# A last column tile computed by two halves of 176 tokens, each with its own norm and output

## Chip, core and metric

The kernel runs on one core of one Trainium2 chip. The metric is the time of one execution in device microseconds (us). Three runs before the change took 1801.14 us in the median (1799.97 to 1801.76).

## What is computed

One layer of a hybrid decoder for 1024 prompt tokens and 32 sample tokens (8 sequences of 4): an input projection shared by four branches, the branches themselves, an output projection with the residual, and a last RMS norm. The change touches only the end of this:

```python
mix = jnp.concatenate([y_ml, y_ssd, y_sc, y_rg], axis=-1)
y = x + mix @ w_out
...
x32 = x.astype(jnp.float32)
y = x32 * lax.rsqrt(jnp.mean(x32 * x32, axis=-1, keepdims=True) + EPS)
return (y * w.astype(jnp.float32)).astype(x.dtype)
```

D is 2048, so the norm of a token needs the token's value in all 2048 features before any of them can be stored.

## The kernel before

The data lie transposed: features on the 128 partitions (16 column tiles n of 128 features), the 1056 tokens along the free axis. `out_proj` (L1322) computes the tokens in two groups. The first has 704 tokens as two chunks of 352, the last has 352 (`GB`). For each of its 16 column tiles the last group's loop (L1404) loads the residual (`begin`, L1336), runs eight steps ke of six matmuls each, and ends with `fin` (L1343): residual added on VectorE (L1351), square on ScalarE (L1358), the squares summed into `acc` (L1359), and the tile scaled by the norm's weight (L1361).

**Three matmuls for one.** For f32 accuracy `mm6` (L278) uses split operands: xh and xl for the data, wh and wl for the weights, each kept in float32r. A step ke has two blocks of 128 rows and for each the lines L282, L283 and L284, every one with its own weight load. In the last group each matmul streams 352 columns.

**The weights.** `weights_list` (L225) lists every weight tile in the order of use. `w_load` (L247) issues the loads on SyncE (L252) into a ring of raw buffers, six in this stage; `w_split` (L255) makes wh with a copy on ScalarE (L264) and wl with a subtraction on VectorE (L265). Eight pairs of split buffers are in use in the last group, four of them regions of xl that are no longer needed. A pair is free again when the six matmuls that read it are done. `w_next` (L268) runs up to seven splits ahead, so the splits of a tile's ke 6 and ke 7 are placed while that tile computes. A raw buffer's next load is placed one split after the split that empties it, and waits for that split's subtraction.

**Order.** The program is written out by hand: each engine executes its instructions in the order in which the code emits them, and an instruction that waits holds up all behind it on that engine. Issuing a DMA occupies its engine's queue too.

**The end.** After the 48 matmuls of the last tile (n = 15) the norm follows once for all 352 tokens: the sum over the partitions of `acc` by matmuls with a column of 1/D (L1423), the last tile's residual and square (L1425, L1426, in two pieces of 128 and 224 tokens), its sum (L1428), square root (L1430), reciprocal (L1431), the result spread over the partitions by transposes into two banks (L1434), a copy of one of them for GpSimd (L1436). Then 16 multiplications, eleven on VectorE (L1443), four on GpSimd (L1441) and the last tile's own (L1439), and one output DMA for each on SyncE (L1444). The square root needs a table of ScalarE, loaded ahead of a dummy at L1419.

Of the kernel before, what the change touches and what calls it, by code (L numbers as in the profile page):

```python
# [12 lines left out]
AF = mybir.ActivationFunctionType  # L13
OP = mybir.AluOpType

D = 2048
KT = 16
TP = 1024
TS = 32
NT = TP + TS  # L20
# [7 lines left out]
GB = CH  # L28
# [80 lines left out]
class Build:  # L109
# [115 lines left out]
    def weights_list(self):  # L225
# [14 lines left out]
        for n in range(KT):  # L240
            for ke in range(8):
                lst.append((o, n, ke))
# [1079 lines left out]
    def out_proj(self):  # L1322
        V, S, G, P, Q = self.V, self.S, self.G, self.P, self.Q
        io = self.io
# [79 lines left out]
        for n in range(KT):  # L1404
# [5 lines left out]
            if n == KT - 1:  # L1410
                break
            fin(n, 1, [(b, w) for b, _, w in ch])

        nb = (GB + 127) // 128
        cut = [(i, slice(128 * i, min(GB, 128 * i + 128)), min(128, GB - 128 * i)) for i in range(nb)]
        tc, rc, mean = self.take(nb), self.take(nb), self.take(2)
# [3 lines left out]
        bs, bk = [self.mx() for _ in cut], self.pj()  # L1420
        y, t, b = ys[1], sq[0], ch[0][0]
        for i, ts, m in cut:
            P.matmul(bs[i][:m, 0:1], acc[1][:, ts], mean[:, 0:1], start=True, stop=False)  # L1423
        for ts in (slice(0, 128), slice(128, GB)):
            V.tensor_add(y[KT - 1][:, ts], b[:, ts], y[KT - 1][:, ts])  # L1425
            S.activation(t[:, ts], y[KT - 1][:, ts], AF.Square)  # L1426
        for i, ts, m in cut:
            P.matmul(bs[i][:m, 0:1], t[:, ts], mean[:, 0:1], start=False, stop=True)  # L1428
        for i, ts, m in cut:
            S.activation(tc[:m, i:i + 1], bs[i][:m, 0:1], AF.Sqrt, bias=self.eps[:m])  # L1430
        V.reciprocal(rc.ap, tc.ap)  # L1431
        bk2 = self.pj()
        for b, (i, ts, m) in [(b, x) for b in (bk, bk2) for x in cut]:
            P.transpose(b[:, ts], rc[:m, i:i + 1].to_broadcast([m, 128]), self.ident[:m, :m])  # L1434
        rb = self.take(GB)
        S.activation(rb.ap, bk2[:, :GB], AF.Copy)  # L1436
        for n in range(KT):
            if n == KT - 1:
                V.scalar_tensor_tensor(y[n], y[n], self.par("fnorm", n), rb.ap, op0=OP.mult, op1=OP.mult)  # L1439
            elif n % 3 == 2 and n < 14:  # L1440
                G.tensor_mul(y[n], y[n], rb.ap)  # L1441
            else:
                V.tensor_mul(y[n], y[n], bk[:, :GB])  # L1443
            Q.dma_start(io["y_out"][n, :, W[0]:NT], y[n])  # L1444
# [141 lines left out]
```

## Time and profile before

| what | value |
|---|---|
| median of three runs | 1801.14 us |
| the profiled execution | 1800.25 us |
| its span, first to last instruction | 1798.5 us |
| mean granted TensorE clock | 0.997 |
| last column tile (1776.58 to 1784.45) | 7.87 us |
| norm, to the first output's issue (1784.45 to 1787.77) | 3.32 us |
| first to last output's issue (1787.77 to 1795.76) | 7.99 us |
| from there to the end | 2.74 us |

Times in the trace count from the first instruction; the 1.75 us between span and execution lie around it. Engines are PE (TensorE; PEld are its weight loads), DVE (VectorE), ACT (ScalarE), POOL (GpSimd), SP (SyncE); a name with q (SPq, ACTq) is that engine's queue issuing a DMA. A merged row of the timeline gives start, length from the first start to the last end, the line, the operation and how many instructions it holds; in brackets stands how long the engine was idle ahead of it and who ended that. Matmuls overlap, so their spacing is read from starts, not from durations.

### The profile page before, as it was taken

What the parts mean: (1) busy time and instruction counts of PE and PEld (TensorE: products, weight loads), DVE (VectorE), ACT (ScalarE), POOL (GpSimd) and SP (SyncE); (2) the same over time, 40 slices, a digit from 0 to 9 for tenths busy, and PEclk for the clock granted to TensorE, in tenths of its full rate; (3) what the DMA queues carried; (4) which work ended last, traced back from release to release, by engine and by line L of the source; (5) the groups of instructions that cost most, each with busy time, mean ns of one, the idle gap of its engine ahead of it and who ended that gap; (6) DMA issues with size and microseconds to landing.
All of it is one profiled execution on the core that took longest, in us unless ns stands there. A gap on an engine that the chain in (4) does not pass through costs nothing.

```text
span 1798.5 us, 30156 instructions
## 1 busy us (share of the span) xinstructions
PE 1782.8 (99%) x11459; PEld 1752.9 (97%) x11459; DVE 910.8 (51%) x2018; ACT 531.7 (30%) x1263; POOL 182.9 (10%) x244
## 2 busy tenths in 40 slices
PE   9999999999999999999999999999999999999997
PEld 8899999999999999999999999999999999999997
DVE  4493454535435444765277556544763633333664
ACT  6522122212212111331144122212441432222453
POOL 1000102011011000320000003100000011110121
PEclk9999999999999999999999999999999999999998
DMA  9411213122122122332212233321123633332774
GB/s 341 146 55 50 78 49 90 50 71 74 58 68 62 53 59 71 91 80 67 80 42 60 63 78 92 69 84 57 57 61 92 202 111 94 94 92 86 216 246 152
DMA packets 141558, 168.19 MB, mean 94 GB/s; under 512 B 18220, under 2 KB 126196, under 8 KB 140900
## 3 DMA queue, kind: packets, MB, share of 16 engines
q1 hardware_dynamic: 135492, 145.36, 28.6%
q0 software_dynamic: 5184, 19.42, 2.8%
q8 instruction: 90, 1.47, 0.3%
q10 hardware_dynamic: 736, 1.48, 0.2%
q14 instruction: 56, 0.46, 0.1%
HBM read 144.35 MB, written 21.84 MB: 92 GB/s over the span
## 4 chain that ended last, share of the span: by engine, by line
PE 91%; issue 6%; DVE 1%; DMA 0%; SPq 0%; ACT 0%; POOL 0%; DVEq 0%; ACTq 0%; POOLq 0%
PE bank L282 29%; PE bank L284 28%; PE bank L283 28%; PE bank L1114 1%; PE bank L498 0%; PE bank L900 0%; PE bank L878 0%; PE bank L899 0%; PE bank L1108 0%; DMA arena<-in_x 0%; PE bank L902 0%; PE bank L1111 0%; PE bank L876 0%; DVE arena L1443 0%; PE bank L1196 0%
## 5 line engine op out<-in xcount | busy, mean ns | idle before, releaser
L282 PE MATMUL bank<-xh,wh 128*128 128x352 f32 x3328 | 1084.6, 326 | 0.5 <-DVE arena L593 0.4
L283 PE MATMUL bank<-xl,wh 128*128 128x352 f32 x3328 | 1072.0, 322 | 1.4 <-DVE xl L474 1.4
L284 PE MATMUL bank<-xh,wl 128*128 128x352 f32 x3328 | 1071.8, 322 | 0.5 <-DVE wl L265 0.5
L282 PEld LDWEIGHTS bank<-xh,wh 128*128 128x128 f32 x3328 | 625.4, 188 | 12.9 <-issue 10.1
L283 PEld LDWEIGHTS bank<-xl,wh 128*128 128x128 f32 x3328 | 626.0, 188 | 2.2 <-DVE xl L474 2.2
L284 PEld LDWEIGHTS bank<-xh,wl 128*128 128x128 f32 x3328 | 626.2, 188 | 1.2 <-DVE wl L265 1.2
L265 DVE TENSOR_TENSOR wl<-wr,wh 128x256 fp32r<-128x256 f32 x568 | 247.9, 447 | 407.2 <-ACT wh L264 404.8
L264 ACT ACTIVATE wh<-wr 128x256 fp32r<-128x256 f32 x568 | 227.1, 413 | 593.7 <-PE bank L283 529.2
L593 DVE TENSOR_TENSOR arena<-bank,arena 128x352 f32<-128x352 f32 x114 | 58.4, 523 | 73.3 <-PE bank L284 72.8
L1359 POOL TENSOR_TENSOR arena<-arena 128x352 f32<-128x352 f32 x39 | 36.8, 948 | 316.0 <-ACT arena L1358 315.8
L944 DVE SCALAR_TENSOR_TENSOR arena<-arena 128x1080 f32<-128x1080 f32 (+1 forms) x44 | 59.9, 1362 | 1.0
L265 DVE TENSOR_TENSOR wl<-arena,wh 128x256 fp32r<-128x256 f32 x72 | 31.5, 451 | 42.3 <-ACT wh L264 42.1
L1358 ACT ACTIVATE arena<-arena 128x352 f32<-128x352 f32 x44 | 21.9, 500 | 68.4 <-DVE arena L1351 66.5
L282 PE MATMUL bank<-xh,xl 128*128 128x352 f32 x128 | 41.5, 324 | 0.0
L284 PE MATMUL bank<-xh,xl 128*128 128x352 f32 x128 | 41.4, 324 | 0.0
L264 ACT ACTIVATE wh<-arena 128x256 fp32r<-128x256 f32 x72 | 28.7, 410 | 42.6 <-PE bank L283 39.9
L283 PE MATMUL bank<-xl 128*128 128x352 f32 x128 | 41.1, 321 | 0.0
L1351 DVE TENSOR_TENSOR arena<-bank,arena 128x352 f32<-128x352 f32 x47 | 24.0, 522 | 32.7 <-PE bank L284 32.6
L586 DVE TENSOR_TENSOR arena<-bank,arena 128x352 f32<-128x352 f32 x32 | 16.4, 522 | 42.4 <-PE bank L284 42.4
L399 DVE RECIPROCAL arena<-arena 128x352 f32<-128x352 f32 (+3 forms) x18 | 35.6, 1980 | 0.2
L474 DVE SCALAR_TENSOR_TENSOR xl<-arena,xh 128x1056 fp32r<-128x1056 f32 (+1 forms) x20 | 21.7, 1095 | 23.3 <-ACT xh L471 23.3
L932 POOL COPY arena<-arena 128x3 f32<-128x3 f32 (+1 forms) x16 | 5.1, 317 | 267.1 <-DVE arena L588 267.1
(340 smaller groups left out, 1253.7 us busy)
## 6 DMA issues: line engine op xcount, KB each, us to landing
wr<-in_w_in SPq DMA_DIRECT2D x438, 128.0 KB
wr<-in_w_out SPq DMA_DIRECT2D x172, 128.0 KB
arena<-in_w_out SPq DMA_DIRECT2D x84, 128.0 KB
arena<-in_xr SPq DMA_DIRECT2D x16, 512.0 KB
arena<-rowd SPq DMA_DIRECT2D x32, 256.0 KB
mixd<-arena POOLq DMA_DIRECT2D x15, 528.0 KB, 3.8
arena<-mixd SPq DMA_DIRECT2D x15, 528.0 KB
arena<-in_x SPq DMA_DIRECT2D x14, 528.5 KB
```

Of the source, the lines that this page charges most:

```text
L264: self.S.activation(h, r, AF.Copy)
L265: self.V.tensor_sub(l, r, h.bitcast(F32))
L282: self.P.matmul(bank[:, :n], wh[:, k, :], xh, start=first and k == 0, stop=False)
L283: self.P.matmul(bank[:, :n], wh[:, k, :], xl, start=False, stop=False)
L284: self.P.matmul(bank[:, :n], wl[:, k, :], xh, start=False, stop=last and k == 1)
L399: self.V.reciprocal(x[:, a:b], x[:, a:b])
L474: V.scalar_tensor_tensor(self.xl[:, k, ts], x, w, self.xh[:, k, ts].bitcast(F32), op0=OP.mult, op1=OP.subtract)
L593: V.tensor_mul(a[:, t0:t0 + CH], bank[:, :CH], rs[:, t0:t0 + CH])
L944: V.scalar_tensor_tensor(y[:, :n], a[:, i:i + n], w(i), y[:, :n], op0=OP.mult, op1=OP.add)
L1351: V.tensor_add(y[:, ts], b[:, :w], y[:, ts])
L1358: S.activation(t, y[:, ts], AF.Square)
L1359: (G if nacc[gr] < KT - 1 else V).tensor_add(a[:, ts], a[:, ts], t)
```

## The change

The last tile of the last group is computed twice over half the tokens: first all eight steps ke for tokens 0 to 175 of the group (h0 below), then all eight for tokens 176 to 351 (h1). The eight weight tiles are listed, loaded and split a second time for h1. The norm is a generator `norm(h, b)` with the same steps for 176 tokens (two cuts of 128 and 48), run up to the reciprocal after h1's ke 1, and the rest (transposes, multiplications, output DMAs of 88 KB) after h1's ke 3. The norm of h1 follows h1's matmuls. Outputs of h0 go out on SyncE, those of h1 on SyncE (even n) and on ScalarE (odd n). The memsets and the dummy square root with its table load now come ahead of the last tile's matmuls.

```diff
-        for n in range(KT):
+        for n in [*range(KT), KT - 1]:
             for ke in range(8):
                 lst.append((o, n, ke))
...
-        for n in range(KT):
+        for n in range(KT - 1):
             begin(n, 1)
...
+        begin(KT - 1, 1)
+        H = GB // 2
+        cuts = [(0, 128), (128, H)]
+        nb = len(cuts)
+        tc, rc, mean, rb = self.take(2 * nb), self.take(2 * nb), self.take(2), self.take(GB)
         V.memset(mean.ap, 1.0 / D)
         V.memset(tc.ap, 1.0)
         S.activation(rc[:, 0:1], tc[:, 0:1], AF.Sqrt)
...
+        def norm(h, b):
+            t = sq[h]
+            bs, bk, bk2 = [self.mx() for _ in cuts], self.pj(), self.pj()
+            for i, (u, v) in enumerate(cuts):
+                P.matmul(bs[i][:v - u, 0:1], acc[1][:, H * h + u:H * h + v], mean[:, 0:1], start=True, stop=False)
+            hs = slice(H * h, H * h + H)
+            V.tensor_add(y[KT - 1][:, hs], b[:, :H], y[KT - 1][:, hs])
+            S.activation(t[:, :H], y[KT - 1][:, hs], AF.Square)
+            for i, (u, v) in enumerate(cuts):
+                P.matmul(bs[i][:v - u, 0:1], t[:, u:v], mean[:, 0:1], start=False, stop=True)
+            for i, (u, v) in enumerate(cuts):
+                S.activation(tc[:v - u, nb * h + i:nb * h + i + 1], bs[i][:v - u, 0:1], AF.Sqrt, bias=self.eps[:v - u])
+            V.reciprocal(rc[:, nb * h:nb * h + nb], tc[:, nb * h:nb * h + nb])
+            yield
+            for bb in (bk, bk2):
+                for i, (u, v) in enumerate(cuts):
+                    P.transpose(bb[:, u:v], rc[:v - u, nb * h + i:nb * h + i + 1].to_broadcast([v - u, 128]),
+                                self.ident[:v - u, :v - u])
+            S.activation(rb[:, hs], bk2[:, :H], AF.Copy)
+            for n in range(KT):
...
+                (S if n % 2 and h else Q).dma_start(io["y_out"][n, :, W[0] + H * h:W[0] + H * h + H], y[n][:, hs])
+
+        hb = [self.pj(), self.pj()]
+        for h in range(2):
+            for ke in range(8):
+                w = self.w_next()
+                self.mm6(hb[h], *w, ke, W[0] + H * h, H, ke == 0, ke == 7)
+                if h and ke == 1:
+                    part = norm(0, hb[0])
+                    next(part)
+                elif h and ke == 3:
+                    for _ in part:
+                        pass
+        for _ in norm(1, hb[1]):
+            pass
```

In the changed kernel the norm's lines are L1426 (sum of `acc`), L1428 (residual), L1429 (square), L1431 (sum of the last tile), L1433 (square root), L1434 (reciprocal), L1438 (transposes), L1440 (copy), L1447, L1445 and L1443 (multiplications on VectorE, GpSimd, and the last tile's) and L1448 (output DMAs).

How the instructions stand on ScalarE from the end of tile 14 on, before (wr, wh and xl are the raw and split weight buffers, the number a buffer's; arena is working memory):

```order
L1361 ACTIVATE arena<-arena 128x352
L264 ACTIVATE xl<-wr_67 128x2x128
L264 ACTIVATE wh_77<-wr_68 128x256
L1419 ACT_TABLE_LOAD
L1419 ACTIVATE arena<-arena 128x1
L1426 ACTIVATE arena<-arena 128x128
L1426 ACTIVATE arena<-arena 128x224
```

The same place after the change:

```order
L1419 ACT_TABLE_LOAD
L1419 ACTIVATE arena<-arena 128x1
L264 ACTIVATE xl<-wr_67 128x2x128
L264 ACTIVATE wh_77<-wr_68 128x256
L264 ACTIVATE wh_71<-wr_69 128x256
L264 ACTIVATE wh_73<-arena 128x256
L264 ACTIVATE wh_75<-arena 128x256
L264 ACTIVATE xl<-wr_70 128x2x128
L264 ACTIVATE xl<-wr_67 128x2x128
L264 ACTIVATE xl<-wr_68 128x2x128
L264 ACTIVATE xl<-wr_69 128x2x128
L264 ACTIVATE wh_77<-arena 128x256
```

The table load and the dummy have moved ahead of the last tile's splits of ke 6 and ke 7 (the first two L264), and the eight splits of h1 follow them. Next on ScalarE comes L1429, the square of h0. On VectorE stands the matching order; after the change, from the first split of h1 on (bank_83 holds h0, bank_85 its spread factors):

```order
L265 TENSOR_TENSOR wl_72<-wr_69,wh_71 128x256
L265 TENSOR_TENSOR wl_74<-arena,wh_73 128x256
L265 TENSOR_TENSOR wl_76<-arena,wh_75 128x256
L265 TENSOR_TENSOR xl<-wr_70,xl 128x2x128
L265 TENSOR_TENSOR xl<-wr_67,xl 128x2x128
L265 TENSOR_TENSOR xl<-wr_68,xl 128x2x128
L265 TENSOR_TENSOR xl<-wr_69,xl 128x2x128
L265 TENSOR_TENSOR wl_78<-arena,wh_77 128x256
L1428 TENSOR_TENSOR arena<-bank_83,arena 128x176
L1434 RECIPROCAL arena<-arena 128x2
L1447 TENSOR_TENSOR arena<-arena,bank_85 128x176 x11
L1443 SCALAR_TENSOR_TENSOR arena<-arena 128x176
```

Before, two L265 and two memsets stood there, and then the residual. Now the residual of h0 (L1428) stands behind all eight subtractions for h1. On SyncE, before, from the load of the last tile's ke 5 on:

```order
L252 DMA wr_70<-in_w_out 128x256
L252 DMA wr_67<-in_w_out 128x256
L252 DMA wr_68<-in_w_out 128x256
L1341 DMA arena<-in_x 128x352
L1444 DMA out_y_out<-arena 128x352 x16
```

After the change:

```order
L252 DMA wr_69<-in_w_out 128x256
L252 DMA arena<-in_w_out 128x256 x2
L1341 DMA arena<-in_x 128x352
L252 DMA wr_70<-in_w_out 128x256
L252 DMA wr_67<-in_w_out 128x256
L252 DMA wr_68<-in_w_out 128x256
L252 DMA wr_69<-in_w_out 128x256
L252 DMA arena<-in_w_out 128x256
L1448 DMA out_y_out<-arena 128x176 x24
```

Eight weight loads have joined, three ahead of the residual's load and five behind it, and SyncE has 24 output DMAs in its queue, 16 of h0 and then eight of h1. ScalarE's queue ends with the other eight.

More of the change, by code (lines that the diff above doesn't have):

```diff
@@ L1409, in out_proj @@
                 self.tick()
-            if n == KT - 1:
-                break
             fin(n, 1, [(b, w) for b, _, w in ch])
-        nb = (GB + 127) // 128
-        cut = [(i, slice(128 * i, min(GB, 128 * i + 128)), min(128, GB - 128 * i)) for i in range(nb)]
-        tc, rc, mean = self.take(nb), self.take(nb), self.take(2)
+        begin(KT - 1, 1)
[3 more added lines that the diff above has]
+        tc, rc, mean, rb = self.take(2 * nb), self.take(2 * nb), self.take(2), self.take(GB)
         V.memset(mean.ap, 1.0 / D)
@@ L1419, in out_proj @@
         S.activation(rc[:, 0:1], tc[:, 0:1], AF.Sqrt)
[L1420 to L1444, printed above, removed]
+        y = ys[1]
@@ new lines, in norm @@
+        def norm(h, b):
[18 more added lines that the diff above has]
+            for n in range(KT):
+                if n == KT - 1:
+                    V.scalar_tensor_tensor(y[n][:, hs], y[n][:, hs], self.par("fnorm", n), rb[:, hs], op0=OP.mult, op1=OP.mult)
+                elif n % 3 == 2 and n < 14:
+                    G.tensor_mul(y[n][:, hs], y[n][:, hs], rb[:, hs])
+                else:
+                    V.tensor_mul(y[n][:, hs], y[n][:, hs], bk[:, :H])
+                (S if n % 2 and h else Q).dma_start(io["y_out"][n, :, W[0] + H * h:W[0] + H * h + H], y[n][:, hs])
```

## Prediction

> **What bounds the kernel now.** First the page: the span, the engines' busy time, the chain that ended last.
>
> ```profile
> span 1798.5 us, 30156 instructions
> ...
> PE 1782.8 (99%) x11459; PEld 1752.9 (97%) x11459; DVE 910.8 (51%) x2018; ACT 531.7 (30%) x1263; POOL 182.9 (10%) x244
> ...
> PE 91%; issue 6%; DVE 1%; DMA 0%; SPq 0%; ACT 0%; POOL 0%; DVEq 0%; ACTq 0%; POOLq 0%
> ```
>
> TensorE bounds the kernel as a whole, but the change touches the last 22 us alone, so the next view is the table of windows for these stages: the last column tile, the norm, the stretch of output issues, the rest.
>
> ```profile
> core 0: us, PE busy (x) PEld busy (x) DVE busy (x) ACT busy (x) POOL busy (x), PEclk, DMA share, GB/s
> 1776.58:1784.45 7.87, 7.87 (x52) 7.87 (x51) 1.83 (x6) 3.19 (x6) 0.00 (x0) 1.00 0.00 1
> 1784.45:1787.77 3.32, 2.21 (x17) 1.79 (x17) 1.32 (x5) 1.58 (x6) 0.00 (x0) 1.00 0.02 5
> 1787.77:1795.76 7.99, 0.00 (x0) 0.00 (x0) 4.77 (x11) 0.22 (x1) 3.60 (x4) 0.53 0.85 306
> 1795.76:1798.50 2.74, 0.00 (x0) 0.00 (x0) 0.00 (x0) 0.00 (x0) 0.00 (x0) 0.50 0.45 159
> ```
>
> TensorE is the limit for 7.87 us, a serial norm takes 3.32 us, and then 10.7 us follow in which TensorE does nothing. What paces those is in the timeline.
>
> ```profile
> 1776.58 0.32 PE L282 MATMUL bank<-xh,wh 128*128 128x352 f32 x1
> ...
> 1784.12 0.32 PE L284 MATMUL bank<-xh,wl 128*128 128x352 f32 x1
> 1784.13 0.74 PEld L1423 LDWEIGHTS bank<-arena 128*128 128x128 f32 x6
> ...
> 1784.48 0.59 DVE L1425 TENSOR_TENSOR arena<-bank,arena 128x128 f32<-128x128 f32 x2 [4.85 <-PE bank L284]
> 1784.86 0.64 ACT L1426 ACTIVATE arena<-arena 128x128 f32<-128x128 f32 x2 [4.21 <-issue]
> ...
> 1785.22 0.88 PE L1428 MATMUL bank<-arena 128*128 128x1 f32 x6 [0.27 <-ACT arena L1426]
> ...
> 1786.66 0.82 PE L1434 MATMUL bank<-arena 128*128 128x128 f32 x6 [0.56 <-DVE arena L1431]
> 1787.22 4.83 DVE L1443 TENSOR_TENSOR arena<-arena,bank 128x352 f32<-128x352 f32 x11 [0.61 <-PE bank L1434]
> ...
> 1787.77 7.99 SPq L1444 DMA_DIRECT2D out_y_out<-arena  x16
> ...
> 1791.97 0.58 DVE L1439 SCALAR_TENSOR_TENSOR arena<-arena 128x352 f32<-128x352 f32 x1
> ```
>
> VectorE has its last result at 1791.97 + 0.58 = 1792.55, but SyncE issues until 1787.77 + 7.99 = 1795.76. So the tail is paced by SyncE, one issue after another, not by the norm or by the multiplications. The next rows give its period: seven output issues together, the durations of one (least, median, most, in ns), three weight issues together, their durations, and the sizes.
>
> ```profile
> 1792.40 3.36 SPq L1444 DMA_DIRECT2D out_y_out<-arena  x7
> ```
> ```profile
> L1444 SPq DMA_DIRECT2D out_y_out<-arena x16: 333/400/411, 1787.8 to 1795.4; - x16
> ```
> ```profile
> 1772.03 1.33 SPq L252 DMA_DIRECT2D wr<-in_w_out  x3
> ```
> ```profile
> L252 SPq DMA_DIRECT2D wr<-in_w_out x10: 328/382/392, 1759.8 to 1773.0; - x10
> ```
> ```profile
> out_y_out<-arena SPq DMA_DIRECT2D x16, 176.0 KB
> wr<-in_w_out SPq DMA_DIRECT2D x3, 128.0 KB
> ```
>
> (3.36 - 0.40) / 6 = 0.49 us from issue to issue at 176 KB; (1.33 - 0.38) / 2 = 0.475 at 128 KB. A quarter fewer bytes, nearly the same period: SyncE pays per DMA. The last issue starts at 1792.40 + 6 x 0.49 = 1795.35; 3.15 us later the span ends.
>
> **The change, part by part.** *The matmuls.* Of 352 columns one follows the other by (1784.12 - 1776.58) / 47 = 0.160 us. 48 become 96 of 176 columns. No such matmul is in the trace; the bounds are half of it, 0.08, and all of it, 0.16. I take 0.11: at L1423, where almost nothing streams, six weight loads take 0.74, (0.74 - 0.17) / 5 = 0.11 from one to the next (0.17 an estimate for the last, narrower one), and each of the 96 brings its own load. [...] With h0 for the first half, TensorE's own chain has h0's 48 and the second half's first 12 done at 1776.58 + 60 x 0.11 = 1783.2, and L1426 at 1783.6. Next in its queue is L1431, which needs h0's square. That is where the first wait is added.
>
> *The splits in front of the norm.* On VectorE and ScalarE h0's add (L1428) and square (L1429) now stand behind all eight weight splits of the second half, and the table load (L1419) ahead of the first tile's last two.
>
> ```profile
> 1777.93 0.59 ACT L1361 ACTIVATE arena<-arena 128x352 f32<-128x352 f32 x1
> 1778.43 0.40 ACT L264 ACTIVATE xl<-wr 128x256 fp32r<-128x256 f32 x1
> 1778.73 0.40 ACT L264 ACTIVATE wh<-wr 128x256 fp32r<-128x256 f32 x1
> 1779.15 1.28 ACT L1419 ACT_TABLE_LOAD   x1
> 1780.45 0.20 ACT L1419 ACTIVATE arena<-arena 128x1 f32<-128x1 f32 x1
> ```
> ```profile
> 1778.86 0.42 DVE L265 TENSOR_TENSOR xl<-wr,xl 128x256 fp32r<-128x256 f32 x1 [0.34 <-ACT xl L264]
> ```
> ```profile
> 1756.60 1.28 SPq L252 DMA_DIRECT2D wr<-in_w_out  x3
> ```
> ```profile
> 1758.88 0.42 ACT L264 ACTIVATE xl<-wr 128x256 fp32r<-128x256 f32 x1 [1.12 <-DMA wr<-in_w_out]
> ```
>
> The table load now starts at 1778.53 and with L1419 ends at 1780.03. The split of ke 6 runs from there: 0.43 to its subtraction (1778.43 to 1778.86), 0.42 for that, done at 1780.89. Six raw buffers serve the loads, so the load of the second half's ke 4 waits for exactly this subtraction. SyncE issues the last four loads from 1780.92, 0.475 apart, ke 7 at 1782.35. From issue to a split that waited on it took 1758.88 - 1756.60 = 2.28 us (the first of the three). So ke 7 is split from 1784.63 and subtracted from 1785.06 to 1785.48. Only now comes L1428. Its cost lies between the two pieces of before:
>
> ```profile
> L1425 DVE TENSOR_TENSOR arena<-bank,arena 128x224 f32<-128x224 f32 x1 | 0.4, 380 | 0.0
> ...
> L1426 ACT ACTIVATE arena<-arena 128x128 f32<-128x128 f32 x1 | 0.3, 310 | 4.2 <-issue 4.2
> ...
> L1425 DVE TENSOR_TENSOR arena<-bank,arena 128x128 f32<-128x128 f32 x1 | 0.3, 292 | 4.8 <-PE bank L284 4.8
> ```
>
> 0.34 for 176 columns, 0.35 for the square, 0.08 and 0.05 of handover (1784.86 and 1785.22 after the ends before them): 1785.40 + 0.82 = 1786.22. TensorE stands at L1431 from 1783.6 until then, 2.6 us, with 36 matmuls behind it. If the splits came in time this wait would be nothing; if the loads took half a microsecond more it would be 3.1.
>
> *From there to the first output.* Four instructions of L1431, 0.44; ke 2 and 3, 12 x 0.11 = 1.32, under which square root and reciprocal hide; L1438 to the first multiplication 0.45 (0.56 for three transposes, 1786.66 to 1787.22, now two): 1788.43. That multiplication's end and the issue: 0.55 before (1787.22 to 1787.77), 0.37 with half the columns. The eight added weight loads are long out on SyncE by then (the last at 1782.35), the eight added splits fill idle time on ScalarE and VectorE. First output issue 1788.80, **1.0 us later than before**, not earlier.
>
> *The issues.* Before, 16 on SyncE; now h0's 16 and eight of the second half, 24, the other eight on ScalarE. h0's multiplications cost about 0.25 each (352 columns: (4.83 - 0.51) / 10 = 0.43; the 128 columns of L1425 0.59 - 0.38 = 0.21), so SyncE is the slower and its queue never empties: h0's sixteenth starts at 1788.80 + 15 x 0.49 = 1796.2. The second half's data are ready by then: 24 matmuls to 1791.1, VectorE free of h0's twelve at 1791.5, 2.6 to its first multiplication (1784.48 to 1787.22 is 2.74), 3.05 for twelve, 1797.2 for the last. The 24th issue starts at 1788.80 + 23 x 0.493 = 1800.14; 3.1 to the end (a little less for half the bytes): 1803.2.
>
> **The sum**: first issue 1788.80 - 1787.77 = +1.03; from first to last issue 23 x 0.493 = 11.34 against 1795.35 - 1787.77 = 7.58, +3.76; the end 3.1 against 3.15, -0.05: **+4.7 us**. The profiled execution took 1800.25 (span 1798.5) and becomes 1804.9; on the median of 1801.14, 0.9 above it, **1805.8**. 0.2%, about what a measurement of this kernel can tell from no change, is 3.6 us.
>
> Bounds of the unknowns: matmuls at 0.08 give -0.4, at 0.16 +1.1 (TensorE reaches L1431 at 1786.8, then 12 x 0.05 more); loads half a microsecond more or less 0.5 either way; the issue 0.475 instead of 0.493 -0.4. The forecast's own range is 1804.3 to 1807.3.
>
> **Rivals.** *The issue goes by bytes (ends on the other side: not slower).* The stretch of 16 issues moves 306 GB/s at a share of 0.85, so its period may be the transfer's, and 88 KB would need less. The end moves by 23p - 6.6: at p below 0.44 the change is not slower by 0.2%, and from 0.37 down the second half's own data decide, 1797.2 + 3.1 = 1800.3, +1.9, 1803.0. For it speaks that stretch; against it the weight loads, 0.475 at 128 KB. 17%.
>
> *The norm of h0 comes as early as the program puts it, and the issue is cheap too.* Then L1431 runs at 1783.6, all that follows is 2.6 earlier, and the second half's own data decide: 1797.2 - 2.6 + 3.1 = 1797.7, -0.8, 1800.3, no change. Both must hold; the order of VectorE speaks against the first. 6%.
>
> *The narrow matmul falls to the rate of plain f32.* The trace has both at 256 columns, two of each:
>
> ```profile
> 751.96 0.59 PE L1108 MATMUL bank<-arena 128*128 128x256 f32 x2
> ```
> ```profile
> 743.73 0.40 PE L1093 MATMUL bank<-fb,fa 96*128 96x256 f32 x2
> ```
>
> Plain f32 needs two instructions for one matmul. Of a matmul's 0.32 the next covers 0.16 (the rows at 1776.58 and 1784.12), so plain f32 costs 0.59 - 0.16 = 0.43 and the fast form (0.40 - 0.16) / 2 = 0.12; at 176 columns plain f32 would be 0.43 x 176 / 256 = 0.29 each, an estimate. L1438 then starts at 1776.58 + 72 x 0.29 + 0.88 = 1798.3; the second half's last matmul ends at 1805.8, its first multiplication starts at 1808.5, SyncE's last issue at 1808.9 + 7 x 0.49 = 1812.3: +17, 1818. For it: the narrowest fast matmul shown has 256 columns. Against it: 352 and 256 columns scale alike. 8%.
>
> *Both queues share one generator.* Then ScalarE's eight save nothing: at 1794.8, when its first data are ready, 12 of SyncE's 24 are out and 20 issues are left, 0.40 each: the last starts at 1802.4, the end is 1805.5, +7.0, 1808.1.
>
> ```profile
> 839.73 0.36 ACTq L321 DMA_DIRECT2D arena<-nrmd  x1
> 839.78 0.33 SPq L252 DMA_DIRECT2D wr<-in_w_in  x1
> ```
>
> Here two issues overlap and neither is longer for it. [...] 5%.
>
> **How the numbers follow.** The forecast has 64%, the rivals 17, 6, 8 and 5. The range 1802.6 to 1809.0 holds the forecast, the bytes case and the shared generator, and leaves out 14%. Slower by over 0.2%: 0.9 of the 64%, 8 and 5, about 0.71. Within: 17, 6 less a little and the rest of the 64%, 0.27. Faster by over 0.2%: 0.02; even both gains together give only 0.8 us.
>
> **What would show it.** Right: about 24 issues on SyncE, 0.49 apart, to some 1800; L1428's first instance after the last L265, near 1785.4; an idle of 2 to 3 us ahead of L1431; 96 matmuls 0.11 apart where nothing waits. Wrong: output issues 0.4 or less apart; L1431 without a wait; narrow matmuls at 0.15 or more, with TensorE busy past 1792.

## The result and the profile after

| kernel | median, us | against before, 95% interval |
|---|---|---|
| before | 1801.14 (1799.97 to 1801.76, 3 runs) | |
| after | 1811.39 (1811.24 to 1812.54, 3 runs) | 1.0057 [1.0043, 1.0072] |

The change costs 10.25 us (0.57%, the interval is clear of no change); 4.7 were forecast. The profiled execution took 1811.39 us, its span is 1809.6. Its last tile starts at 1776.99, 0.41 later than before; that offset arises ahead of the change.

First the page of after. TensorE is busy for 10.8 us more than before; the chain that ended last has nearly the same shares.

```profile
span 1809.6 us, 30366 instructions
...
PE 1793.6 (99%) x11513; PEld 1762.3 (97%) x11513; DVE 916.8 (51%) x2039; ACT 535.5 (30%) x1273; POOL 183.4 (10%) x248
...
PE 91%; issue 6%; DVE 1%; DMA 1%; ACT 0%; POOL 0%; SPq 0%; DVEq 0%; ACTq 0%; POOLq 0%
```

The table of windows has one row a stage: h0's matmuls with h1's first 12; h0's sums; TensorE's wait; from L1431 to h0's first output issue; to h1's last matmul; h1's norm to its first issue on SyncE; its issues; the rest.

```profile
core 0: us, PE busy (x) PEld busy (x) DVE busy (x) ACT busy (x) POOL busy (x), PEclk, DMA share, GB/s
1776.99:1783.80 6.81, 6.81 (x63) 6.75 (x61) 3.26 (x10) 4.58 (x11) 0.00 (x0) 1.00 0.34 97
1783.80:1784.29 0.49, 0.49 (x6) 0.38 (x4) 0.20 (x1) 0.26 (x1) 0.00 (x0) 1.00 0.82 268
1784.29:1788.24 3.95, 0.00 (x0) 0.00 (x0) 1.75 (x5) 1.60 (x4) 0.00 (x0) 0.69 0.09 26
1788.24:1792.76 4.52, 4.52 (x20) 3.93 (x20) 0.53 (x3) 0.51 (x2) 0.00 (x0) 0.50 0.00 0
1792.76:1798.18 5.42, 5.42 (x26) 5.33 (x26) 3.02 (x11) 0.32 (x1) 2.12 (x4) 0.50 0.48 150
1798.18:1801.72 3.54, 2.71 (x13) 1.97 (x12) 0.87 (x4) 0.85 (x3) 0.00 (x0) 0.50 0.56 178
1801.72:1806.54 4.82, 0.27 (x2) 0.11 (x1) 3.01 (x11) 0.32 (x1) 2.10 (x4) 0.50 0.65 205
1806.54:1809.60 3.06, 0.00 (x0) 0.00 (x0) 0.00 (x0) 0.00 (x0) 0.00 (x0) 0.50 0.45 148
```

Two things stand out. TensorE is idle for 3.95 us, and within that time its granted clock falls (column PEclk) from 1.00 to 0.50, where it stays to the end. Before, the clock fell at 1788.27, when TensorE's work was done (its last row, the transposes of 1786.66, ends at 1787.48). The timeline of TensorE:

```profile
1783.80 0.49 PE L1426 MATMUL bank<-arena 128*128 128x1 f32 x4
1788.24 0.84 PE L1431 MATMUL bank<-arena 128*128 128x1 f32 x4 [3.96 <-ACT arena L1429]
...
1789.54 0.41 PE L284 MATMUL bank<-xh,wl 128*128 128x176 f32 x1
1789.75 0.41 PE L282 MATMUL bank<-xh,wh 128*128 128x176 f32 x1
...
1791.67 1.36 PE L1438 MATMUL bank<-arena 128*128 128x128 f32 x4
...
1797.96 0.41 PE L284 MATMUL bank<-xh,wl 128*128 128x176 f32 x1
```

Up to the wait the narrow matmuls come 0.111 us apart (of the steps between the first 60, two are longer, 0.17 and 0.19); behind it they come 0.2135 apart, and this holds for h1's remaining 36. Who made TensorE wait is in the timelines of SyncE's queue and ScalarE: h1's loads of ke 3 to 6 in one row and of ke 7 in the next, then the splits of ke 4 to 7, then h0's square.

```profile
1776.13 6.39 SPq L252 DMA_DIRECT2D wr<-in_w_out  x4
1782.61 0.38 SPq L252 DMA_DIRECT2D arena<-in_w_out  x1
```
```profile
1783.64 0.42 ACT L264 ACTIVATE xl<-wr 128x256 fp32r<-128x256 f32 x1 [1.35 <-DMA wr<-in_w_out]
1784.30 0.97 ACT L264 ACTIVATE xl<-wr 128x256 fp32r<-128x256 f32 x2 [0.24 <-PE bank L1426]
1786.63 0.42 ACT L264 ACTIVATE wh<-arena 128x256 fp32r<-128x256 f32 x1 [1.36 <-DMA arena<-in_w_out]
1787.84 0.35 ACT L1429 ACTIVATE arena<-arena 128x176 f32<-128x176 f32 x1 [0.79 <-DVE arena L1428]
```

The last load, issued at 1782.61, is split at 1786.63, 4.02 us later; its subtraction, h0's add and the square follow, and TensorE goes on at 1788.24. The last view is the output issues: SyncE's first fourteen, its three around the change from h0 to h1, and the durations of one on both queues (least, median, most, in ns).

```profile
1792.76 6.89 SPq L1448 DMA_DIRECT2D out_y_out<-arena  x14
```
```profile
1799.74 2.32 SPq L1448 DMA_DIRECT2D out_y_out<-arena  x3
```
```profile
L1448 SPq DMA_DIRECT2D out_y_out<-arena x24: 332/382/413, 1792.8 to 1806.0; - x24
...
L1448 ACTq DMA_DIRECT2D out_y_out<-arena x8: 338/390/413, 1802.1 to 1806.2; - x8
```

(6.89 - 0.38) / 13 = 0.50 us a DMA of 88 KB. The three would take 1.4 us in a row and take 2.32: SyncE ran out of data when h0's sixteen were out, because h1 was not ready.

### The profile page after: what moved, and what is told of

Read it like the earlier page. It is cut to its first block, busy times and chain, and to the rows that moved or that the text cites. A ratio compares the mean times of both kernels' runs of the same rounds, so it can differ in the third digit from the quotient of the medians.

```text
span 1809.6 us, 30366 instructions
## 1 busy us (share of the span) xinstructions
PE 1793.6 (99%) x11513; PEld 1762.3 (97%) x11513; DVE 916.8 (51%) x2039; ACT 535.5 (30%) x1273; POOL 183.4 (10%) x248
## 4 chain that ended last, share of the span: by engine, by line
PE 91%; issue 6%; DVE 1%; DMA 1%; ACT 0%; POOL 0%; SPq 0%; DVEq 0%; ACTq 0%; POOLq 0%
PE bank L282 29%; PE bank L284 28%; PE bank L283 28%; PE bank L1114 1%; PE bank L498 0%; PE bank L900 0%; PE bank L878 0%; PE bank L899 0%; PE bank L1108 0%; DMA arena<-in_x 0%; PE bank L902 0%; PE bank L1111 0%; PE bank L876 0%; DMA wr<-in_w_in 0%; DMA arena<-in_w_out 0%
## 5 line engine op out<-in xcount | busy, mean ns | idle before, releaser
L265 DVE TENSOR_TENSOR wl<-wr,wh 128x256 fp32r<-128x256 f32 x569 | 248.6, 448 | 409.6 <-ACT wh L264 408.6
L264 ACT ACTIVATE wh<-wr 128x256 fp32r<-128x256 f32 x569 | 227.7, 413 | 597.5 <-PE bank L283 530.6
L265 DVE TENSOR_TENSOR wl<-arena,wh 128x256 fp32r<-128x256 f32 x75 | 32.8, 451 | 44.1 <-ACT wh L264 43.5
L282 PE MATMUL bank<-xh,xl 128*128 128x352 f32 (+1 forms) x136 | 44.5, 327 | 0.0
L284 PE MATMUL bank<-xh,xl 128*128 128x352 f32 (+1 forms) x136 | 44.5, 327 | 0.0
L283 PE MATMUL bank<-xl 128*128 128x352 f32 (+1 forms) x136 | 44.1, 324 | 0.0
L264 ACT ACTIVATE wh<-arena 128x256 fp32r<-128x256 f32 x75 | 29.8, 410 | 43.9 <-PE bank L283 38.3
L265 DVE TENSOR_TENSOR xl<-wr,xl 128x256 fp32r<-128x256 f32 x46 | 19.1, 423 | 26.2 <-ACT xl L264 24.8
```

Source lines behind the costliest of these rows:

```text
L264: self.S.activation(h, r, AF.Copy)
L265: self.V.tensor_sub(l, r, h.bitcast(F32))
L282: self.P.matmul(bank[:, :n], wh[:, k, :], xh, start=first and k == 0, stop=False)
L283: self.P.matmul(bank[:, :n], wh[:, k, :], xl, start=False, stop=False)
L284: self.P.matmul(bank[:, :n], wl[:, k, :], xh, start=False, stop=last and k == 1)
```

## The experiments

**The theory** they test: (a) TensorE waits at L1431 because h0's add and square stand behind h1's splits, whose last load lands late; (b) the wait halves the clock and h1 pays for it; (c) only without both do the 24 issues of SyncE decide, as the forecast had it. **Rivals**: the issues alone; the narrow matmuls, or the second load and split of the weights, by themselves.

In six of the fourteen traces (e2_keep, e5_table_late, e6_rewarm, e7_before_act, e8_early_warm, e11_late_early) the clock falls once near the start, far ahead of the change, as these windows of e2_keep show. All that follows comes about 2 us later (the last tile starts at 1779.22 in e2_keep, at 1776.41 in e9_keep_act). So where traces are compared, times count from the last tile's first matmul ("+").

```profile
13.72:17.13 3.41, 1.22 (x7) 0.80 (x6) 1.62 (x2) 2.69 (x4) 0.00 (x0) 1.00 1.05 375
17.13:20.54 3.41, 3.41 (x13) 3.41 (x12) 3.25 (x5) 1.70 (x3) 2.86 (x5) 0.50 0.92 308
```

| kernel | median, us | against before, 95% interval | L1431 starts | first issue | end |
|---|---|---|---|---|---|
| before | | | | +11.19 | +21.92 |
| after | 1811.39 | 1.0057 [1.0043, 1.0072] | +11.25 | +15.77 | +32.6 |
| e1_warm | 1807.80 | 1.0038 [1.0025, 1.0050] | +11.72 | +14.48 | +29.2 |
| e2_keep | 1804.99 | 1.0018 [1.0009, 1.0027] | +7.22 | +9.99 | +24.7 |
| e3_act | 1811.65 | 1.0059 [1.0046, 1.0071] | +11.31 | +15.82 | +33.0 |
| e4_early | 1808.60 | 1.0041 [1.0028, 1.0054] | +8.95 | +12.98 | +29.8 |
| e5_table_late | 1809.87 | 1.0043 [1.0029, 1.0057] | +8.56 | +12.80 | +29.7 |
| e7_before_act | 1801.69 | 0.9999 [0.9991, 1.0008] | | | |
| e8_early_warm | 1805.70 | 1.0027 [1.0018, 1.0036] | +9.20 | +11.97 | +28.2 |
| e9_keep_act | 1802.72 | 1.0011 [1.0002, 1.0020] | +7.23 | +9.99 | +23.6 |
| e11_late_early | 1803.48 | 1.0016 [1.0007, 1.0025] | +7.43 | +10.19 | +24.9 |
| e12_late_early_act | 1802.59 | 1.0014 [1.0005, 1.0023] | +7.48 | +10.24 | +24.0 |

Each ratio is against runs of the kernel before that were made along with that kernel's own; their medians differ by up to 1.2 us, so the ratios are compared, not the medians. e6_rewarm and e10_rewarm_narrow ran once each (1815.28 and 1821.46 us): their fillers cost time, and only their traces are of use.

### The clock: e1_warm

```diff
+            for i in range(24 if h == 0 else 0):
+                P.matmul(self.bank[7][:, :CH], self.xh[:, i % KT, 0:128], self.xh[:, i % KT, W[0]:NT], start=True, stop=True)
             hs = slice(H * h, H * h + H)
             V.tensor_add(y[KT - 1][:, hs], b[:, :H], y[KT - 1][:, hs])
```

> The changed kernel with 24 filler matmuls of 352 columns on TensorE between L1426 and L1431 of h0 (24 x 0.16 = 3.85 us, the length of the idle time there); their results go to an unused bank and are not read. Theory (the idle time of 3.95 us before L1431 lowers the granted clock from 1.00 to 0.50, and the rest of the kernel pays for it): L1431 still at about 1788.2, but the clock stays near 1.0, the 36 matmuls of h1 that are left come 0.111 apart and not 0.2135, h0's first output is issued near 1790.8 and not 1792.76, h1's last matmul starts near 1793 and not 1798.2; then the 24 issues of SyncE decide (1790.8 + 24 x 0.497 + 3.06), span near 1805.8, some 4 us under the changed kernel. Rival 1 (the clock is not what counts, the late start of h0's output is): no gain, or slower by what the fillers delay. Rival 2 (the issues decide already): the gain is only what the first issue comes earlier, about 2 us.

The windows of e1_warm: the fillers, from h0's L1431 to the first issue, to h1's last matmul.

```profile
1784.00:1788.27 4.27, 3.86 (x25) 3.58 (x24) 1.58 (x5) 1.45 (x4) 0.00 (x0) 1.00 0.06 18
1788.27:1791.03 2.76, 2.76 (x21) 2.38 (x21) 0.53 (x3) 0.44 (x2) 0.00 (x0) 1.00 0.00 0
1791.03:1793.75 2.72, 2.72 (x26) 2.72 (x25) 2.72 (x11) 0.32 (x1) 2.13 (x4) 1.00 0.42 132
```

The span is 1805.8, as the theory had it. Nothing was done but to keep TensorE busy while it waits. L1431 comes no earlier (+11.72 against +11.25), yet the next two stretches fall from 4.52 to 2.76 and from 5.42 to 2.72 us. From 1.0057 to 1.0038 the clock's share is about 3.4 us. SyncE's 24 issues now run without a gap (1791.03, 11.66 us long), so they decide, and of the 4.5 us that TensorE wins here the end keeps the part that they leave.

### No second load and split: e2_keep

```diff
-        for n in [*range(KT), KT - 1]:
+        for n in range(KT):
...
-                w = self.w_next()
+                if h == 0:
+                    ws.append(self.w_next(ke == 0))
+                    self.low = 0
+                w = ws[ke]
```

(`low` lets `w_split` fill the eighth pair of split buffers as well.)

> The changed kernel, but h1 uses the eight split weight pairs of h0 again: the second load and the second split of the last tile's weights are gone. Theory (L1431 waits because h0's add stands behind h1's splits, whose last load lands late): no wait before L1431 (near 1784.4), clock near 1.0 throughout, h0's first issue near 1786.9; then 24 SyncE issues of 0.497 decide: span near 1786.9 + 11.9 + 3.1 = 1801.9, that is 7.7 us under the changed kernel and 2 to 3 us above the kernel before. Rival 1 (the cost is in the narrow matmuls themselves, 96 of them 0.111 apart in place of 48 at 0.16): the matmuls are all still here, so at most 2 us are won. Rival 2 (SyncE's issues do not decide even then): h1's data are ready near 1795, span near 1798.5, 11 us under the changed kernel and faster than the kernel before.

L1431 at +7.22 without a wait, first issue +9.99, 24 issues in a row, end +24.7; had the last tile started at 1776.55, as in e1_warm, the span would be 1801.2. So with (a) and (b) gone the forecast's own term is left, about 3 us above before. The span was 1803.9 where 1801.9 was expected, because of the shift near the start, shown above.

### Output issues on two queues: e3_act and e9_keep_act

e3_act changes the line of the output DMAs in the changed kernel, e9_keep_act in e2_keep:

```diff
-                (S if n % 2 and h else Q).dma_start(io["y_out"][n, :, W[0] + H * h:W[0] + H * h + H], y[n][:, hs])
+                (S if n % 2 else Q).dma_start(io["y_out"][n, :, W[0] + H * h:W[0] + H * h + H], y[n][:, hs])
```
```diff
-                (S if n % 2 and h else Q).dma_start(io["y_out"][n, :, W[0] + H * h:W[0] + H * h + H], y[n][:, hs])
+                (S if n % 2 and (h or n < 8) else Q).dma_start(io["y_out"][n, :, W[0] + H * h:W[0] + H * h + H], y[n][:, hs])
```

> The changed kernel with h0's odd outputs issued by ScalarE too (16 issues on SyncE and 16 on ScalarE in all, in place of 24 and 8). Theory (h1's own data set the end, since its matmuls and norm run at half the clock): no gain, within 0.7 us of the changed kernel; SyncE waits for h1's data longer than before. If ScalarE's eight early issues hold up h1's square L1429, somewhat slower. Rival (the 24 issues in a row on SyncE set the end, as the forecast had it): up to 8 x 0.497 = 4 us faster.

> The kernel e2_keep with four of h0's outputs (n = 1, 3, 5, 7) issued by ScalarE, so that SyncE has 20 issues in a row in place of 24. Theory (once the wait and the half clock are gone, the 24 issues of SyncE set the end, which is the forecast's last term): 4 x 0.497 = 2.0 us under e2_keep if nothing else comes late, and not less than 1 us; the last output is then set by h1's data and its 16 issues on two queues. Rival (transfers or h1's data set the end in e2_keep already): no gain, as in e3_act.

The timelines of the issues, e3_act first, then e9_keep_act:

```profile
1792.11 13.51 SPq L1448 DMA_DIRECT2D out_y_out<-arena  x16
1792.43 4.48 ACTq L1448 DMA_DIRECT2D out_y_out<-arena  x8
1801.45 4.51 ACTq L1448 DMA_DIRECT2D out_y_out<-arena  x8
```
```profile
1786.40 10.47 SPq L1449 DMA_DIRECT2D out_y_out<-arena  x20
1786.65 2.17 ACTq L1449 DMA_DIRECT2D out_y_out<-arena  x4
1792.37 4.31 ACTq L1449 DMA_DIRECT2D out_y_out<-arena  x8
```

The same edit does nothing in the changed kernel (1.0059 against 1.0057), where h0's outputs are out at 1796.9 and the queues then wait for h1 until 1801; and gains 1.1 us in the trace where the clock is kept (the intervals of 1.0018 and 1.0011 overlap, so the times alone don't show it). In the changed kernel the issues decide nothing; behind the repaired wait they do. The gain stayed under the 2.0 of four issues, since SyncE's last issue is then only 0.2 us behind ScalarE's (1796.54 and 1796.32): h1's 16 issues on two queues, about 0.55 apart on each, from 1792.4, are the bound that follows.

### The order on VectorE and ScalarE: e4_early and e5_table_late

```diff
             S.activation(t[:, :H], y[KT - 1][:, hs], AF.Square)
+            yield
...
-                if h and ke == 1:
+                if h == 0 and ke == 7:
                     part = norm(0, hb[0])
                     next(part)
+                elif h and ke == 1:
+                    next(part)
```

> The changed kernel with h0's add L1428 and square L1429 written right behind h0's last matmul, so that on VectorE and ScalarE they stand ahead of the splits of h1's last two weight pairs (ke 6 and 7); the sums on TensorE stay where they were. Theory: L1431 near 1785.5 after an idle time of about 1.2 us in place of 3.95, the clock stays near 1.0, h1's last weights are split while TensorE works on h1's ke 2 to 6, first issue near 1788.9, h1 ready early enough, so that the 24 issues decide: span near 1788.9 + 11.9 + 3.1 = 1803.9, some 5.6 us under the changed kernel. Rival (h1's late last weights are what counts, wherever the add stands): TensorE then waits at h1's ke 7 instead, and the clock falls there; gain under 2 us.

```diff
-        S.activation(rc[:, 0:1], tc[:, 0:1], AF.Sqrt)
...
                 w = self.w_next()
+                if h == 0 and ke == 5:
+                    S.activation(rc[:, 0:1], tc[:, 0:1], AF.Sqrt)
```

> The changed kernel with one instruction moved: the square root that brings in ScalarE's table (L1419) is written behind the last tile's matmuls of ke 5 of h0, so that the table load of 1.28 us stands behind the splits of h1's first four weight pairs and not ahead of the last tile's splits. Theory (the wait before L1431 comes from h1's last load; it is issued late because the splits that free its buffer stand behind the table load, and it then meets the packet of 16 KB on queue q8 at 1783.3 to 1784.4): the four loads are issued 1.3 to 1.6 us earlier and land before that packet, the last one 2.3 to 2.7 us after its issue and not 4.0 to 4.5; the idle time before L1431 falls from 3.95 to about 1 us; the clock stays near 1.0; h0's first output is issued near 1787.8 and the 24 issues decide: span near 1802.8, about 6.8 us under the changed kernel. Rival 1 (the packet on q8 has no part in it): the last load still takes 4 us, the idle time is 2.4 us, the clock falls, gain 1.5 to 2.5 us. Rival 2 (the table load only moves to where it delays the last splits): no gain.

Each shortens the wait as far as the theory has it or nearly (1.49 and 1.41 us in place of 3.95), and in each the clock falls all the same, so each gains less than expected: 2.9 us in place of 5.6, and about 2.5 in place of 6.8 (from the ratios). The theory's "the clock stays near 1.0" is wrong for both. TensorE at the end of the wait in e5_table_late, then in e4_early, then e4_early's two windows on both sides of the fall:

```profile
1787.00 0.56 PE L1430 MATMUL bank<-arena 128*128 128x1 f32 x4 [1.41 <-ACT arena L1428]
```
```profile
1785.45 0.56 PE L1432 MATMUL bank<-arena 128*128 128x1 f32 x4 [1.49 <-ACT arena L1429]
```
```profile
1782.80:1786.21 3.41, 1.92 (x17) 1.73 (x16) 1.26 (x4) 1.79 (x5) 0.00 (x0) 1.00 0.36 101
1786.21:1789.62 3.41, 3.41 (x16) 2.82 (x15) 1.19 (x6) 0.45 (x3) 0.00 (x0) 0.50 0.00 0
```

In e4_early the clock falls at 1786.21, when TensorE has been at work again for 0.76 us. Between two changes of the clock the traces have whole multiples of 3.4133 us: it is full for 522 of them before (6.52 to 1788.27), for 521 after (7.43 to 1785.77), and half for two in e6_rewarm (1788.29 to 1795.12). So the traces are read here in stretches of this length, counted from the changes of the clock; as the times show, they lie elsewhere in each execution. That the clock goes by what went on in the stretch ahead, and not by the idle time as such, is a reading and was not tested by itself.

e5_table_late answers the part about the load. SyncE's issue of the last load, and its split on ScalarE:

```profile
1782.55 0.38 SPq L252 DMA_DIRECT2D arena<-in_w_out  x1
```
```profile
1785.39 0.42 ACT L264 ACTIVATE wh<-arena 128x256 fp32r<-128x256 f32 x1 [0.28 <-DMA arena<-in_w_out]
```

It takes 2.84 us in place of 4.02. In the trace's packets of the changed kernel one of 16 KB on queue q8 (the page of the profile calls it instruction) starts at 1784.33 and takes 0.95 us. All weight packets but eight are done by 1784.84; the eight start when the 16 KB are through, at 1785.26, one after the other, about 0.11 us apart, until 1786.06. That the eight waited for the 16 KB is read from these times; the trace does not say what they waited for. In e3_act the last load is as late (issued at 1781.91, split at 1785.99, 4.08 us), and the DMA engines are 0.81 busy in 1783.0 to 1783.5 and 0.03 to 0.06 in 1784.0 to 1785.5. The packet could not be moved alone, so its part is shown by coincidence only.

### What sets the clock: e6_rewarm and e10_rewarm_narrow

e6_rewarm places 24 fillers of 352 columns behind h0's L1431, e10_rewarm_narrow 48 of 176. The edit of e6_rewarm:

```diff
                 P.matmul(bs[i][:v - u, 0:1], t[:, u:v], mean[:, 0:1], start=False, stop=True)
+            for i in range(24 if h == 0 else 0):
+                P.matmul(self.bank[7][:, :CH], self.xh[:, i % KT, 0:128], self.xh[:, i % KT, W[0]:NT], start=True, stop=True)
```

> The changed kernel with 24 filler matmuls of 352 columns on TensorE behind L1431 of h0, that is after the clock has fallen; their results go to an unused bank and are not read. It asks why the clock stays at 0.50 while h1's 36 matmuls of 176 columns run for over 9 us without a gap. Theory (the clock comes back after one stretch of about 3.4 us that is filled with wide matmuls, as at the start of the program, and 176 columns per matmul do not fill it): the fillers begin 0.32 apart, the clock returns to 1.0 within 3.4 to 6.8 us of their start, the last of them are 0.16 apart and h1's 36 matmuls 0.111 apart. Rival (once lowered, the clock stays lowered this late, or needs far longer): all 24 are 0.32 apart and h1's matmuls 0.2135 apart. The time by itself says nothing, since the fillers take 4 to 8 us.

> The kernel e6_rewarm with 48 fillers of 176 columns in place of 24 of 352: the same columns through TensorE, in twice as many matmuls; their results are not read. Theory (the clock rises after a stretch of 3.4 us in which at least about 3500 columns went through, ten matmuls of 352; at half the clock matmuls of 176 columns come 0.2135 apart, 16 in a stretch, 2816 columns): the clock stays at 0.50 through all 48 fillers, about 10 us, and through h1. Rival (TensorE being busy without a gap is enough, whatever the width; in the changed kernel it was only not long enough): the clock rises during the fillers, as it did in e6_rewarm after two stretches.

Windows by stretches of 3.41 us, e6_rewarm first, then e10_rewarm_narrow:

```profile
1788.29:1791.70 3.41, 1.78 (x7) 1.75 (x8) 0.84 (x3) 1.27 (x4) 0.00 (x0) 0.50 0.00 0
1791.70:1795.12 3.42, 3.42 (x13) 3.42 (x13) 0.00 (x0) 0.00 (x0) 0.00 (x0) 0.50 0.00 0
1795.12:1798.53 3.41, 3.41 (x26) 3.16 (x24) 0.10 (x1) 0.00 (x0) 0.00 (x0) 1.00 0.00 0
```
```profile
1789.48:1792.90 3.42, 3.42 (x18) 3.42 (x18) 0.00 (x0) 0.00 (x0) 0.00 (x0) 0.50 0.00 0
1792.90:1796.31 3.41, 3.41 (x18) 3.41 (x18) 0.00 (x0) 0.00 (x0) 0.00 (x0) 0.50 0.00 0
1796.31:1799.72 3.41, 3.41 (x18) 3.41 (x18) 0.00 (x0) 0.00 (x0) 0.00 (x0) 0.50 0.00 0
```

The clock is full again at the end of the first stretch that the wide fillers fill (1795.12); through the narrow ones it stays at 0.50 for 10.2 us, with TensorE just as busy. So it is not busy time that counts here. What goes along with the clock is the number of columns of all matmuls that start in a stretch. Counted in the traces before and after, from the clock's first record on, every stretch with 2512 columns or fewer has half the clock in the next one, and every one with 4224 or more has the full clock; none lies between. The low ones all lie at the end of the two programs. The reverse case is in the trace before: from 13.34 to 16.76 TensorE is busy for only 2.19 of 3.42 us, but 4224 columns start, and the clock stays full. Twelve wide matmuls at half the clock are 4224 columns (the second stretch of e6_rewarm above, with the full clock behind it); sixteen narrow ones, 0.2135 apart, are 2816 (the three of e10_rewarm_narrow, all at half). At full clock 30 narrow ones make 5280 (after, 1778.94 to 1782.36), and the next stretch has it too. The changed kernel does not recover: from 1785.77 on its stretches have at most 2512 columns.

### A shorter wait and fillers: e8_early_warm

e4_early with nine fillers of 352 columns ahead of L1431 of h0.

> The kernel e4_early with 9 filler matmuls of 352 columns ahead of h0's L1432 (9 x 0.16 = 1.44 us, the idle time of 1.49 us there); their results are not read. In e4_early the clock fell although the idle time was 1.49 us. Theory (what counts is how much of a stretch of about 3.4 us TensorE is busy, and 1.5 us of idle time with narrow matmuls around it are enough to lower the clock): the clock stays near 1.0, h0's sums at the same time as in e4_early, first issue near 1788.2, h1's matmuls 0.111 apart, the 24 issues decide: span near 1803.2, 3 us under e4_early. Rival (the clock falls for another reason, such as the narrow matmuls alone): the clock falls all the same, no gain.

The ratio improves from 1.0041 to 1.0027, but in the trace the clock falls even so, one stretch later:

```profile
1784.07:1787.49 3.42, 3.42 (x27) 3.16 (x25) 1.67 (x5) 0.94 (x3) 0.00 (x0) 1.00 0.58 147
1787.49:1790.90 3.41, 3.17 (x24) 2.73 (x24) 1.55 (x6) 1.57 (x6) 0.00 (x0) 1.00 0.00 2
1790.90:1794.31 3.41, 3.41 (x18) 3.41 (x18) 2.44 (x10) 0.04 (x1) 2.12 (x4) 0.50 0.50 159
```

1787.49 to 1790.90 has 0.24 us of idle time and only 2996 columns, for it holds the one-column sums, the transposes and no more than fifteen narrow matmuls. The theory as written (busy time) failed here; the count goes along with the clock, as in the stretch ahead (5280 columns, full clock behind it).

### Order alone: e11_late_early and e12_late_early_act

e11_late_early has the edits of both e4_early and e5_table_late; e12_late_early_act has besides them the issues of e9_keep_act.

> The changed kernel with the edits of e4_early and e5_table_late together, order alone: table load behind the splits of h1's first four weight pairs, h0's add and square ahead of the splits of h1's ke 6 and ke 7. Every load, split, matmul and output of the changed kernel is still there. Counted from the last tile's first matmul, as the other numbers here: theory (the wait before L1431 is a matter of order alone, the second load and split of the weights cost nothing by themselves): no idle time over 0.3 us before L1431, which starts at +7.2 to +7.6 (in the changed kernel +11.25, in e2_keep +7.2), first issue near +10.0, the 24 issues decide, end near +24.8 as in e2_keep (+24.7), 7 to 8 us under the changed kernel (+32.6), about 3 us over the kernel before. If the clock falls in the stretch around L1431 all the same (it has few columns per 3.4 us there, as in e8_early_warm): end at +27 to +28.5. Rival (the second load and split cost something in any order): L1431 waits 1 us or more, end later than +28.

> The kernel e11_late_early with four of h0's outputs (n = 1, 3, 5, 7) issued by ScalarE, as in e9_keep_act. Theory: 1.1 us under e11_late_early, as e9_keep_act stood to e2_keep (ends at +23.6 and +24.7), which leaves it 1 to 2 us above the kernel before (ends at +21.9). Rival (ScalarE has its splits and squares to do at that time and issues late): no gain over e11_late_early.

L1431 in e11_late_early on TensorE, without a bracket (no wait), and the outputs on SyncE:

```profile
1785.23 0.27 PE L284 MATMUL bank<-xh,wl 128*128 128x176 f32 x1
1785.62 0.56 PE L1431 MATMUL bank<-arena 128*128 128x1 f32 x4
```
```profile
1788.38 11.65 SPq L1448 DMA_DIRECT2D out_y_out<-arena  x24
```

The end is +24.9 where +24.8 was expected: every load, split and matmul of the change is there, and with their order mended some 7.4 of its 10.3 us are gone (1.0016 against 1.0057). e12_late_early_act ends 0.9 earlier still in the trace (1.1 expected), which the two intervals can't tell apart. In the trace of e11_late_early the clock holds up to the first issue (1.00 from 1778.19 to 1788.38); in that of e12_late_early_act its mean is 0.998, against 0.993 in the changed kernel. Since the stretches lie elsewhere in each execution, and 0.24 us of idle time went with a fall in e8_early_warm, one trace does not show that the clock holds in all.

### What there was to win: e7_before_act

```diff
-            Q.dma_start(io["y_out"][n, :, W[0]:NT], y[n])
+            (S if n % 2 else Q).dma_start(io["y_out"][n, :, W[0]:NT], y[n])
```

> The kernel before with its odd output tiles issued by ScalarE, 8 issues on SyncE and 8 on ScalarE in place of 16 on SyncE. It asks what the kernel before had left to win in the stretch that the change is about. Theory (in the last 3.7 us of issues the DMA engines are 0.98 busy at 353 GB/s, so that the transfers set the end as well): gain of 0 to 1 us. Rival (SyncE's 16 issues set it): the last issue comes right behind the last multiplication, 1792.5 in place of 1795.35, gain 2.5 us or more.

No gain. The last issue does come earlier, 6.68 us behind the first multiplication in place of 8.13, but the end comes 11.16 behind it in place of 11.26. In the last stretch of issues of e7_before_act the DMA engines are full, as the theory had it:

```profile
1795.90:1798.65 2.75, 0.00 (x0) 0.00 (x0) 0.48 (x1) 0.00 (x0) 0.00 (x0) 0.50 0.98 348
```

So the forecast's reading of the kernel before, "the tail is paced by SyncE, one issue after another", was half of it: the transfers are a second bound right behind. No version here beats the kernel before; the nearest are e9_keep_act and e12_late_early_act. They issue their first output 1.0 to 1.2 us earlier (+9.99 and +10.24 against +11.19). But h1's first multiplication comes at +15.35 in e9_keep_act, where the first of the kernel before, for all tokens, came at +10.64. Those 4.7 us are 96 matmuls at 0.111 in place of 48 at 0.160 (3.0 us), and h0's sums and transposes between them (0.4, 0.5 and 0.8) ahead of h1's norm. From there the end is 8.2 us away, in the kernel before 11.3, since only half of the output is left. The 3.1 us gained do not make up for the 4.7.

## Why the prediction was right and wrong

The sign and the place of the loss were right, the size was not: one wait was taken too short, and what the wait does to the clock was put at nothing.

**Right.** The sign and the place: h0's add behind all eight splits of h1, TensorE stopped at L1431, h0's first output later than before and not earlier. L1431 waited, so the rival of an early norm falls. The narrow matmul was taken at 0.11 and measured 0.111, so the rival of plain f32 falls, and with it the bound of 0.08. The issue goes by the DMA and not by the byte (0.50 us at 88 KB, 0.49 at 176), which ends the rival of bytes. The rival that both queues share one generator falls too: the eight issues of ScalarE and eight of SyncE overlap in 1802 to 1806, and none is longer than 0.41 (the rows of durations above). The last term of the sum, 24 issues in a row on SyncE, did not decide in the changed kernel; it does in e2_keep and e11_late_early, which end at +24.7 and +24.9, 1.9 and 1.7 below the forecast's +26.6, because their first issue is 2 us earlier.

**Wrong, step one: "From issue to a split that waited on it took 2.28 us".** For the last load it took 4.02. The loads were issued as forecast (1782.61, 0.41 of it the offset, against 1782.35), L1431 came at +11.25 in place of +9.64, a wait of 3.95 in place of 2.6. Of the 1.6 us too little, nearly all is this load. The row behind the 2.28 was of the first of three loads, this is the last of four. As the last of four it took 2.84 in e5_table_late; the other 1.18 fall in the time of the packet on q8, and whether it caused them was not shown.

**Wrong, step two: all durations behind the wait were taken at full clock.** "12 x 0.11 = 1.32" for ke 2 and 3 became 2.66, the sums of L1431 0.77 in place of 0.44, the transposes up to the first multiplication 0.72 in place of 0.45. The first issue came at +15.77, 3.55 later than the forecast's +12.22, of which 1.61 is the load and 1.9 these three. e1_warm, where L1431 comes as late but the clock is kept, goes from L1431 to the first issue in 2.76 where the changed kernel takes 4.52, so nearly all of the 1.9 is the clock. The column PEclk was quoted in the forecast and never applied to the wait. The clock did not need the late load to fall. Two stretches of the changed kernel, up to the fall and from it on:

```profile
1782.36:1785.77 3.41, 1.93 (x19) 1.82 (x17) 1.93 (x5) 1.25 (x3) 0.00 (x0) 1.00 0.53 151
1785.77:1789.18 3.41, 0.94 (x5) 0.91 (x6) 0.68 (x2) 1.08 (x4) 0.00 (x0) 0.50 0.00 1
```

The first ends 1.48 us into the wait and has 2116 columns. A wait of 2.6 us, as forecast, would have left it as it is. The clock also fell with a wait of 1.49 in e4_early, with 1.41 in e5_table_late, and with 0.24 us of idle time in a stretch of 2996 columns in e8_early_warm.

**Wrong, step three, by that: "SyncE is the slower and its queue never empties".** h1's 24 matmuls behind the transposes took 5.2 us at 0.2135 and its norm slowed too; its first multiplication, in the forecast 2.6 behind 1791.5, at 1794.1, came at 1801.36. SyncE stood from 1800.6 to 1801.7, and h1's own data set the end. e3_act shows that issues then count for nothing.

The measured end (+32.6) against the forecast's (+26.6), part by part: 1.6 for the load, 1.9 up to the first issue, and 2.4 from there to the end, 16.8 us in place of 14.4. In e1_warm this last part takes 14.75 (+14.48 to +29.23), so 2.1 of the 2.4 go with the clock; 0.3 were too little in the forecast at full clock as well.

**Open.** Whether the packet on q8 causes the late landing was not isolated. Where between 2996 columns (e8_early_warm, half the clock behind them) and 4224 (before and e6_rewarm, full) the change lies was not tried, and the 3500 in the expectation of e10_rewarm_narrow is an estimate; nor was it tried whether the clock goes by the columns or by something that goes with them: no experiment varied the columns alone.

## What to carry to other kernels

Where a change puts work on an engine that waits, price that wait in the clock too: look at PEclk on both sides of it (here 1.00 and 0.50) and at what TensorE streams around it, including the little sums and transposes of a norm. The matmuls of 176 columns held a full clock here (0.111 us apart in e2_keep) and did not win back a lost one (0.2135 apart to the end of the changed kernel), so one stall ahead of them nearly doubled what was left on TensorE. When a step is split in two, what is placed ahead of its first half on the other engines matters more than the second half's extra work: here order alone took back some 7 of 10 us. It still did not pay, because the narrow matmuls and the second norm bring the last half's data later by more than the half sent ahead saves, and spreading the issues gained nothing before, with the DMA engines 0.98 busy.

## What the runs showed of the hardware

- The granted clock was full for 521 times 3.4133 us in the changed kernel (7.43 to 1785.77 us) and for 522 times before, and half for twice 3.4133 us in e6_rewarm. Behind every stretch of this length with at most 2512 matmul columns started it was 0.50 in these two kernels, behind 2996 too (e8_early_warm), behind 4224 and more 1.00. That columns are what is counted is the reading that fits, not one tested by itself.
- In the changed kernel a 176-column matmul with its own weight load came every 0.111 us at a granted clock of 1.00 and every 0.2135 at 0.50.
- In the changed kernel a packet of 16 KB on queue q8 took 0.95 us; eight packets of 1 KB of the weight load under way started as it ended, one after the other, seven of them 0.10 to 0.14 us long, where most take 0.05. The split of that load started 0.57 us after the last of them, 1.8 after all the others were done.
- Output issues on SyncE and ScalarE ran side by side in the changed kernel (1802 to 1806), 0.38 and 0.39 us in the median, none longer than 0.41.
